# Transposes of a hybrid decoder layer, issued in groups of two tiles with the last formed operand first

## The chip, the cores and the metric

One core of a Trainium2 chip runs the whole layer. The metric is the device time of one execution in microseconds (us).

## What is computed

One macaron layer over 1024 prompt tokens and 64 sample tokens, model width 1024, float32:

```
x = x + 1/2 * post1(SwiGLU_1(pre1(x)))          # width 2816, RMS norms pre and post
h = pre_mix(x); z = h @ w_in + b_in
  A: sliding-window attention, 8 heads on 2 key heads of 64, window 128, learned sinks
  B: HGRN2 gated linear recurrence, 4 heads of 128
x = x + post_mix(concat(norm(attn), gate(hgrn)) @ w_out)
x = x + 1/2 * post2(SwiGLU_2(pre2(x)))
```

## The kernel before

**Tiling.** The tokens go in three blocks: n=0 (256 prompt and 64 sample tokens, width 320), n=1 and n=2 (384 each). A product in float32 is made of three matmuls on operands split into a rounded and a rest part, hi by hi, hi by lo, lo by hi (`mm3`, L245 to L247), 320, 384 or 512 columns wide; these are the large matmuls. Weights come by a DMA that SP issues (L229), and `split` forms hi by a cast on ACT (L222) and lo by a subtraction on DVE (L223). Activations stored in DRAM by the first feed-forward come back in the same way: a DMA `ar<-fa` (L966), the cast and the subtraction `h<-ar` (L222, L223).

**Stages.** Feed-forward 1; then for each block the projection `w_in`, attention and recurrence, the projection `w_out`; feed-forward 2. Feed-forward 2 of block 0 is worked on while blocks 1 and 2 are still mixed: a pair of products is taken through `silu` on ACT (L696) and a product on DVE (L702), which free the two banks.

**Where the transposes stand.** `pre_n` (from L404) normalises a block for the mix and transposes x into feature tiles: eight tiles, each three transposes of 128 x 128 into one PSUM bank `tr` (L428), read out by ACT (L432, hi) and DVE (L433, lo). `pre_s` (from L468) does the same for feed-forward 2 of blocks 1 and 2 (L490; read out by ACT, L495, or DVE, L493, in turn; then a cast of four tiles, L509). `attn_block` (from L1177) works on 128 queries in two passes of two heads of each key head: scores `sc` (L1193), a mask and maximum on DVE (L1201), exponentials on ACT (L1210), then for each key head the transposes of the probabilities into a bank `pT` (L1219, four of 128 x 128, two in the first block), read out by DVE for the first key head and by ACT for the second (L1222), then the product with the values `pv` (L1234). Its result is scaled (L1244) and `finish_attn` squares it on ACT (L1164) and transposes it (`oT`, L1172). `hgrn_block` has its own small products (`kT` L1363, `av` L1368 and L1371, `u` L1374), the squares of `finish_hgrn` (L1339) and the update of the state (L1379).

**What sets the order.** All PSUM is eight banks: four with the tag `mm` for large products, four with the tag `ax` for everything else, each handed out in turn; a writer waits until the last reader of its bank's earlier tile is done. The generators above are advanced between large products by `tick`, `pace` and `stream`: each `yield` ends a slot. The resulting program is then scheduled when it is built (`schedule_with_timeline_sim=True`): a simulated timeline puts the instructions of each engine in order, and on the chip each engine works through its list in that order and waits where an operand or a buffer isn't there. SP's list of DMA issues is such a list too.

Of the kernel before, what the change touches and what calls it, by code (L numbers as in the profile page):

```python
# [8 lines left out]
F32 = mybir.dt.float32  # L9
# [4 lines left out]
AF = mybir.ActivationFunctionType  # L14
ALU = mybir.AluOpType
# [3 lines left out]
P = 128  # L19
D = 1024  # L20
KC = D // P
# [23 lines left out]
def tile_step(ctx: ExitStack, tc: tile.TileContext, A: dict, O: dict):  # L45
    nc = tc.nc
    V, S, G, PE = nc.vector, nc.scalar, nc.gpsimd, nc.tensor
# [8 lines left out]
    def uid(s):  # L56
        cnt[0] += 1
        return f"{s}_{cnt[0]}"
# [4 lines left out]
    def axbank(s="ax"):  # L63
        return ps.tile([P, 512], F32, tag="ax", bufs=4, name=uid(s))
# [5 lines left out]
    def big(dt=F32, shape=(P, 4, 384)):  # L70
        return pp.tile(list(shape), dt, tag="big", bufs=10, name=uid("big"))
# [77 lines left out]
    ident = cp.tile([P, P], F32, name="ident")  # L149
# [68 lines left out]
    def small():  # L218
        return pp.tile([P, 4, 8], F32, tag="small", bufs=10, name=uid("sm"))
# [32 lines left out]
    def hcol(h, k, w):  # L252
        return h[0][k // 4][:, k % 4, :w], h[1][k // 4][:, k % 4, :w]
# [6 lines left out]
    def proj_tok(banks, wt, h, n, ks):  # L260

        for i, bank in enumerate(banks):
            r = rows_of(n, i)
            for k2, k in enumerate(ks):
                hh = hcol(h, k, WIDTH[n])
                mm3(bank[:r], (hh[0][:, i * P:i * P + r], hh[1][:, i * P:i * P + r]),
                    (wt[0][:, k2], wt[1][:, k2]), k == 0, k == KC - 1)

    def rows_of(n, i):
        return min(P, WIDTH[n] - i * P)  # L270

    def new_h(n):
        return [[hslot(n), hslot(n)], [hslot(n), hslot(n)]]
# [130 lines left out]
    def pre_n(n, y, gpre, h):  # L404

        w = WIDTH[n]
        sm = small()
        row_rms(n, y, [0, 1, 2], sm)
        yield
        yield  # L410
        yield
        yield
        for i in range(3):
            r = rows_of(n, i)
            for hf in range(2):
                t = y[hf][:r, i]
                if hf:
                    S.activation(t, t, AF.Copy, scale=sm[:r, 1, i:i + 1])
                else:
                    V.tensor_scalar(t, t, sm[:r, 1, i:i + 1], None, op0=ALU.mult)  # L420
        yield
        yield
        h[n] = new_h(n)
        for d in range(KC):
            bank = axbank("tr")
            for i in range(3):
                r = rows_of(n, i)
                PE.transpose(bank[:, i * P:i * P + r], y[d // 4][:r, i, (d % 4) * P:(d % 4) * P + P],  # L428
                             ident[:r, :r])
            hi, lo = hcol(h[n], d, w)  # L430
            g = gpre[:, d:d + 1]
            S.activation(hi, bank[:, :w], AF.Copy, scale=g)  # L432
            V.scalar_tensor_tensor(lo, bank[:, :w], g, hi.bitcast(F32), op0=ALU.mult, op1=ALU.subtract)  # L433
            if d % 2:
                yield

    def pre_x(n, y, gpre, part, f):

# [29 lines left out]
    def pre_s(n, y, gpre, part, f):  # L468


        sm = small()
        row_rms(n, y, [0, 1, 2], sm)
        yield
        for i in range(3):
            for hf in range(2):
                t = y[hf][:, i]
                if hf:
                    S.activation(t, t, AF.Copy, scale=sm[:, 1, i:i + 1])
                else:
                    V.tensor_scalar(t, t, sm[:, 1, i:i + 1], None, op0=ALU.mult)  # L480
            yield

        part[n] = []
        for kh in range(2):
            a = big()
            part[n].append(a)
            for k in range(4):
                bank = axbank("tr")
                for i in range(3):
                    PE.transpose(bank[:, i * P:(i + 1) * P], y[kh][:, i, k * P:(k + 1) * P], ident)  # L490
                g = gpre[:, 4 * kh + k:4 * kh + k + 1]
                if k % 2:
                    V.tensor_scalar(a[:, k], bank[:, :384], g, None, op0=ALU.mult)  # L493
                else:
                    S.activation(a[:, k], bank[:, :384], AF.Copy, scale=g)  # L495
                yield
            if n == 1:
                yield from factor(f, 1 + kh, a)
        if n == 2:
            yield from factors(n, part, f)  # L500
# [542 lines left out]
    def mixing(tp, h):  # L1043
# [132 lines left out]
        def attn_block(n, b):  # L1176
            zq, kx, vn = Z[n]["q"], KX[n], VN[n]  # L1177
            first = n == 0 and b == 0
            nk = 1 if first else 2
            k0 = P if first else b * P  # L1180
            wk = nk * P
            mask = amask[:, P:] if first else amask
            sm, mx = small(), small()
            ob = None

            def of(x, pr):
                return x.rearrange("p (g r i) -> p g r i", g=2, r=2)[:, :, pr]

            for pr in range(2):
                pt, banks = [], [axbank("sc") for _ in range(2)]  # L1190
                for i in range(2):
                    for g in range(2):
                        PE.matmul(banks[g][:, i * 256:i * 256 + wk],  # L1193
                                  zq[64 * g:64 * g + 64, 2 * pr + i, b * P:(b + 1) * P],
                                  kx[64 * g:64 * g + 64, k0:k0 + wk], start=True, stop=True)
                for g in range(2):
                    p = t2((P, 2, 256))
                    pt.append(p)
                    for i in range(2):
                        hd = 4 * g + 2 * pr + i  # L1200
                        V.tensor_tensor_reduce(out=p[:, i, :wk], in0=banks[g][:, i * 256:i * 256 + wk], in1=mask,  # L1201
                                               op0=ALU.add, op1=ALU.max, scale=1.0, scalar=NEG,
                                               accum_out=mx[:, 0, hd:hd + 1])
                V.scalar_tensor_tensor(of(sm[:, 0], pr), of(mx[:, 0], pr), 0.125, of(sinkb, pr),
                                       op0=ALU.mult, op1=ALU.max)
                V.tensor_scalar(of(sm[:, 1], pr), of(sm[:, 0], pr), -1.0, None, op0=ALU.mult)
                for g in range(2):
                    for i in range(2):
                        hd = 4 * g + 2 * pr + i
                        S.activation(pt[g][:, i, :wk], pt[g][:, i, :wk], AF.Exp, bias=sm[:, 1, hd:hd + 1],  # L1210
                                     scale=0.125, accum_out=mx[:, 1, hd:hd + 1])
                yield
                yield
                pT = []
                for g in range(2):
                    bank = axbank("pT")
                    for i in range(2):
                        for kb in range(nk):
                            PE.transpose(bank[:, (i * nk + kb) * P:(i * nk + kb + 1) * P],  # L1219
                                         pt[g][:, i, kb * P:(kb + 1) * P], ident)  # L1220
                    t = t2()
                    (S.copy if g else V.tensor_copy)(t[:, :2 * wk], bank[:, :2 * wk])  # L1222
                    pT.append(t)
                yield
                if ob is None:
                    ob = axbank("pv")
                for i in range(2):
                    for g in range(2):
                        c = (2 * pr + i) * P + 64 * g
                        for kb in range(nk):  # L1230
                            vb = b + kb + (1 if first else 0)
                            for q0 in (0, 64):
                                k1 = (i * nk + kb) * P + q0
                                PE.matmul(ob[q0:q0 + 64, c:c + 64], pT[g][:, k1:k1 + 64],  # L1234
                                          vn[:, vb, g * 64:g * 64 + 64], start=kb == 0, stop=kb == nk - 1)
                if pr == 0:
                    yield
            V.tensor_tensor(sm[:, 2], sinkb, sm[:, 0], op=ALU.subtract)
            S.activation(sm[:, 2], sm[:, 2], AF.Exp)
            V.tensor_tensor(mx[:, 2], mx[:, 1], sm[:, 2], op=ALU.add)  # L1240
            V.reciprocal(mx[:, 3], mx[:, 2])
            yield
            o = t2()
            V.tensor_tensor(o.rearrange("p (m g d) -> p m g d", m=4, g=2),  # L1244
                            ob.rearrange("p (m g d) -> p m g d", m=4, g=2),
                            mx[:, 3].rearrange("p (g m) -> p m g", g=2).unsqueeze(3).to_broadcast([P, 4, 2, 64]),
                            op=ALU.mult)
            yield from finish_attn(n, o, P, slice(b * P, (b + 1) * P))
# [334 lines left out]
    h = {}  # L1583
# [142 lines left out]
    with tc.tile_pool(name="f2", bufs=1) as tp:  # L1726
# [10 lines left out]
        y, sm = f2.ys[1], small()  # L1737
# [77 lines left out]
```

## Time and profile before

| what | us |
|---|---|
| median of 3 runs | 1953.73 (1953.61 to 1954.24) |
| profiled execution | 1954.31 |
| its span | 1952.6 |
| PE busy | 1937.5 (99%) |
| DVE busy | 1349.6 (69%) |
| ACT busy | 929.0 (48%) |
| POOL busy | 211.1 (11%) |

The profiled execution is 1.7 us longer than the span of its trace, and its mean granted clock of TensorE is 0.998. In the chain of work that ended last, PE has 94%, the rest being DMA 2%, DVE 2%, ACT 1% and issue 1%. In the rows below a line of a timeline begins with the start in us and the duration in us; "x4" is four instructions of one kind in a row, whose duration runs from the first start to the last end. A number in square brackets is the idle time of that engine just before, with what ended it. PE's ends are modelled, so steps from start to start are what counts there. A matmul in full float32 (sc, pv, av, u) shows as two records; a transpose as one.

### The profile page before, as it was taken

What the parts mean: (1) busy time and instruction counts of PE and PEld (TensorE: products, weight loads), DVE (VectorE), ACT (ScalarE), POOL (GpSimd) and SP (SyncE); (2) the same over time, 40 slices, a digit from 0 to 9 for tenths busy, and PEclk for the clock granted to TensorE, in tenths of its full rate; (3) what the DMA queues carried; (4) which work ended last, traced back from release to release, by engine and by line L of the source; (5) the groups of instructions that cost most, each with busy time, mean ns of one, the idle gap of its engine ahead of it and who ended that gap; (6) DMA issues with size and microseconds to landing.
All of it is one profiled execution on the core that took longest, in us unless ns stands there. A gap on an engine that the chain in (4) does not pass through costs nothing.

```text
span 1952.6 us, 34158 instructions
## 1 busy us (share of the span) xinstructions
PE 1937.5 (99%) x13451; PEld 1825.4 (93%) x13451; DVE 1349.6 (69%) x2188; ACT 929.0 (48%) x1637; POOL 211.1 (11%) x213
## 2 busy tenths in 40 slices
PE   9999999999999999999999999999999999999998
PEld 9999999999998987788899898999999999999887
DVE  5876667776558666875667765745987877655666
ACT  6633333444445544654345455745544444444453
POOL 0000000000004112111232431101000000000202
PEclk9999999999999999999999999999999999999999
DMA  9643345556677555675434333556555645577974
GB/s 322 209 143 129 144 162 186 179 183 208 236 236 228 163 146 163 213 228 153 120 101 141 115 112 117 190 166 206 174 204 187 217 177 186 206 237 232 308 260 141
DMA packets 162492, 362.65 MB, mean 186 GB/s; under 512 B 16524, under 2 KB 60236, under 8 KB 162316
## 3 DMA queue, kind: packets, MB, share of 16 engines
q1 hardware_dynamic: 161324, 358.65, 55.5%
q8 instruction: 105, 1.72, 0.4%
q10 hardware_dynamic: 1008, 1.84, 0.3%
q14 instruction: 55, 0.45, 0.1%
HBM read 283.78 MB, written 77.63 MB: 185 GB/s over the span
## 4 chain that ended last, share of the span: by engine, by line
PE 94%; DMA 2%; DVE 2%; ACT 1%; issue 1%; POOL 0%; SPq 0%; DVEq 0%; POOLq 0%; ACTq 0%
PE mm L245 28%; PE mm L247 28%; PE mm L246 28%; PE c L247 1%; PE c L245 1%; PE c L246 1%; DMA ar<-fa 1%; PE pv L1234 1%; PE sc L1193 1%; PE pT L1219 1%; PE lv L1267 0%; DMA raw<-in_ffn_w_gu_dram 0%; DMA x1N<-big 0%; PE av L1368 0%; DMA big<-in_x0T_dram 0%
## 5 line engine op out<-in xcount | busy, mean ns | idle before, releaser
L245 PE MATMUL mm<-h,wsph 128*128 128x320 f32 (+1 forms) x1280 | 409.5, 320 | 0.2 <-DVE sg L702 0.2
L247 PE MATMUL mm<-h,wspl 128*128 128x320 f32 (+1 forms) x1280 | 403.5, 317 | 1.2 <-DVE wspl L223 1.2
L246 PE MATMUL mm<-h,wsph 128*128 128x320 f32 (+1 forms) x1280 | 404.4, 316 | 0.0
L223 DVE TENSOR_TENSOR wspl<-raw,wsph 128x1024 fp32r<-128x1024 f32 x200 | 250.0, 1251 | 156.4 <-ACT wsph L222 156.0
L222 ACT CAST wsph<-raw 128x1024 fp32r<-128x1024 f32 x200 | 209.3, 1048 | 270.6 <-PE mm L246 205.4
L222 ACT CAST w<-raw 128x512 fp32r<-128x512 f32 (+1 forms) x226 | 169.3, 754 | 240.3 <-PE mm L246 119.8
L223 DVE TENSOR_TENSOR w<-raw,w 128x512 fp32r<-128x512 f32 (+1 forms) x226 | 196.6, 874 | 87.8 <-ACT w L222 87.3
L245 PEld LDWEIGHTS mm<-h,wsph 128*128 128x128 f32 x1280 | 240.4, 188 | 5.4 <-issue 3.2
L247 PEld LDWEIGHTS mm<-h,wspl 128*128 128x128 f32 x1280 | 239.9, 188 | 3.0 <-DVE wspl L223 1.7
L246 PEld LDWEIGHTS mm<-h,wsph 128*128 128x128 f32 x1280 | 240.5, 188 | 1.5 <-issue 0.7
L245 PE MATMUL mm<-h,w 128*128 128x384 f32 x704 | 235.6, 335 | 0.0
L246 PE MATMUL mm<-h,w 128*128 128x384 f32 x704 | 235.6, 335 | 0.0
L247 PE MATMUL mm<-h,w 128*128 128x384 f32 x704 | 230.5, 335 | 0.0
L245 PE MATMUL mm<-w,h 128*128 128x512 f32 x462 | 182.2, 398 | 1.9 <-DVE big L979 1.0
L246 PE MATMUL mm<-w,h 128*128 128x512 f32 x462 | 181.0, 392 | 0.0
L247 PE MATMUL mm<-w,h 128*128 128x512 f32 x462 | 178.9, 392 | 0.0
L216 POOL TENSOR_TENSOR sm<-sm,mhalf 128x3 f32<-128x3 f32 (+4 forms) x37 | 33.7, 913 | 1187.6 <-DVE sm L304 462.3
L245 PEld LDWEIGHTS mm<-h,w 128*128 128x128 f32 x704 | 132.2, 188 | 0.2 <-ACT big L793 0.2
L222 ACT CAST w<-t 128x512 fp32r<-128x512 f32 x176 | 107.3, 621 | 52.4 <-PE mm L247 46.9
L246 PEld LDWEIGHTS mm<-h,w 128*128 128x128 f32 x704 | 132.1, 188 | 0.0
L247 PEld LDWEIGHTS mm<-h,w 128*128 128x128 f32 x704 | 131.7, 188 | 0.0
L223 DVE TENSOR_TENSOR w<-t,w 128x512 fp32r<-128x512 f32 x176 | 119.0, 687 | 10.5 <-ACT w L222 10.3
(348 smaller groups left out, 3688.5 us busy)
## 6 DMA issues: line engine op xcount, KB each, us to landing
raw<-in_ffn_w_gu_dram SPq DMA_DIRECT2D x154, 512.0 KB
raw<-in_ffn_w_down_dram SPq DMA_DIRECT2D x74, 512.0 KB
raw<-in_w_in_dram SPq DMA_DIRECT2D x54, 512.0 KB
ar<-fa SPq DMA_DIRECT2D x70, 384.0 KB
big<-in_ffn_w_down_dram SPq DMA_DIRECT2D x88, 256.0 KB
fb<-big SPq DMA_DIRECT2D x44, 512.0 KB
raw<-fb SPq DMA_DIRECT2D x40, 512.0 KB
fa<-big SPq DMA_DIRECT2D x22, 768.0 KB
```

Of the source, the lines that this page charges most:

```text
L216: G.tensor_tensor(y, x, mhalf[:y.shape[0], :y.shape[1]], op=ALU.pow)
L222: formed[1] = S.copy(hi, src)
L223: return (lo_eng or V).tensor_tensor(lo, src, hi.bitcast(F32), op=ALU.subtract)
L245: PE.matmul(out, a[0], b[0], start=first, stop=False, skip_group_check=resume)
L246: PE.matmul(out, a[0], b[1], start=False, stop=False, skip_group_check=resume)
L247: r = latest[0] = PE.matmul(out, a[1], b[0], start=False, stop=last, skip_group_check=resume)
L1193: PE.matmul(banks[g][:, i * 256:i * 256 + wk], zq[64 * g:64 * g + 64, 2 * pr + i, b * P:(b + 1) * P], kx[64 * g:64 * g + 64, k0:k0 + wk], ...
L1219: PE.transpose(bank[:, (i * nk + kb) * P:(i * nk + kb + 1) * P], pt[g][:, i, kb * P:(kb + 1) * P], ident)
L1234: PE.matmul(ob[q0:q0 + 64, c:c + 64], pT[g][:, k1:k1 + 64], vn[:, vb, g * 64:g * 64 + 64], start=kb == 0, stop=kb == nk - 1)
```

## The change

A helper `group` takes a list of transposes and issues them from the last to the first, all but the first with the constraint that they be scheduled behind the one issued first. `pre_n` and `pre_s` take two `tr` banks at once and issue the six transposes of two feature tiles as one group; `attn_block` takes both `pT` banks at once and issues the transposes of both key heads as one group, the second key head first. The reading out is as before, behind the group. In `pre_s` the two yields of a pair now stand together behind it; the number of slots is the same in all three.

```diff
--- before.py
+++ after.py
@@ -266,6 +266,13 @@
                 mm3(bank[:r], (hh[0][:, i * P:i * P + r], hh[1][:, i * P:i * P + r]),
                     (wt[0][:, k2], wt[1][:, k2]), k == 0, k == KC - 1)
 
+    def group(ops):
+        ins = None
+        for out, src, eye in reversed(ops):
+            with tc.issue_after(ins) if ins is not None else nullcontext():
+                r = PE.transpose(out, src, eye)
+            ins = ins or r.ins
+
     def rows_of(n, i):
         return min(P, WIDTH[n] - i * P)
 
@@ -421,18 +428,16 @@
         yield
         yield
         h[n] = new_h(n)
-        for d in range(KC):
-            bank = axbank("tr")
-            for i in range(3):
-                r = rows_of(n, i)
-                PE.transpose(bank[:, i * P:i * P + r], y[d // 4][:r, i, (d % 4) * P:(d % 4) * P + P],
-                             ident[:r, :r])
-            hi, lo = hcol(h[n], d, w)
-            g = gpre[:, d:d + 1]
-            S.activation(hi, bank[:, :w], AF.Copy, scale=g)
-            V.scalar_tensor_tensor(lo, bank[:, :w], g, hi.bitcast(F32), op0=ALU.mult, op1=ALU.subtract)
-            if d % 2:
-                yield
+        for d0 in range(0, KC, 2):
+            banks = [axbank("tr") for _ in range(2)]
+            group([(banks[k][:, i * P:i * P + P], y[d0 // 4][:, i, (d0 % 4 + k) * P:(d0 % 4 + k) * P + P], ident)
+                   for k in range(2) for i in range(3)])
+            for k, bank in enumerate(banks):
+                hi, lo = hcol(h[n], d0 + k, w)
+                g = gpre[:, d0 + k:d0 + k + 1]
+                S.activation(hi, bank[:, :w], AF.Copy, scale=g)
+                V.scalar_tensor_tensor(lo, bank[:, :w], g, hi.bitcast(F32), op0=ALU.mult, op1=ALU.subtract)
+            yield
 
     def pre_x(n, y, gpre, part, f):
 
@@ -484,15 +489,17 @@
         for kh in range(2):
             a = big()
             part[n].append(a)
-            for k in range(4):
-                bank = axbank("tr")
-                for i in range(3):
-                    PE.transpose(bank[:, i * P:(i + 1) * P], y[kh][:, i, k * P:(k + 1) * P], ident)
-                g = gpre[:, 4 * kh + k:4 * kh + k + 1]
-                if k % 2:
-                    V.tensor_scalar(a[:, k], bank[:, :384], g, None, op0=ALU.mult)
-                else:
-                    S.activation(a[:, k], bank[:, :384], AF.Copy, scale=g)
+            for k0 in (0, 2):
+                banks = [axbank("tr") for _ in range(2)]
+                group([(bank[:, i * P:(i + 1) * P], y[kh][:, i, (k0 + k) * P:(k0 + k + 1) * P], ident)
+                       for k, bank in enumerate(banks) for i in range(3)])
+                for k, bank in enumerate(banks):
+                    g = gpre[:, 4 * kh + k0 + k:4 * kh + k0 + k + 1]
+                    if k:
+                        V.tensor_scalar(a[:, k0 + k], bank[:, :384], g, None, op0=ALU.mult)
+                    else:
+                        S.activation(a[:, k0 + k], bank[:, :384], AF.Copy, scale=g)
+                yield
                 yield
             if n == 1:
                 yield from factor(f, 1 + kh, a)
@@ -1211,15 +1218,12 @@
                                      scale=0.125, accum_out=mx[:, 1, hd:hd + 1])
                 yield
                 yield
-                pT = []
+                pT, banks = [], [axbank("pT") for _ in range(2)]
+                group([(banks[g][:, (i * nk + kb) * P:(i * nk + kb + 1) * P], pt[g][:, i, kb * P:(kb + 1) * P], ident)
+                       for g in range(2) for i in range(2) for kb in range(nk)])
                 for g in range(2):
-                    bank = axbank("pT")
-                    for i in range(2):
-                        for kb in range(nk):
-                            PE.transpose(bank[:, (i * nk + kb) * P:(i * nk + kb + 1) * P],
-                                         pt[g][:, i, kb * P:(kb + 1) * P], ident)
                     t = t2()
-                    (S.copy if g else V.tensor_copy)(t[:, :2 * wk], bank[:, :2 * wk])
+                    (S.copy if g else V.tensor_copy)(t[:, :2 * wk], banks[g][:, :2 * wk])
                     pT.append(t)
                 yield
                 if ob is None:
```

In the changed kernel the lines lie lower down: the transposes are L273, the reading out L438, L439, L499, L501 and L1226, `ar<-fa` L973, silu L703, pv L1238.

The order of the instructions on all engines is the same in both kernels up to about 824 us of the timeline of before, but for the reversed order inside the groups, and again from about 1420 us on. The number of matmuls is the same. Counted over PE's whole order, the runs of small matmuls between large ones go from 147 to 126.

The first place is at about 829 us, where a product of feed-forward 1 that is still open takes a stored activation (`h_1142`, from the load `ar_1143`) while weights of `w_in` (`raw_1184`) are loaded. SP's DMA issues, before and now:

```order
L966 DMA ar_1128_8081<-fa1_101 128x2x384
L229 DMA raw_1166_8354<-in_w_in_dram 128x1024
L229 DMA raw_1179_8414<-in_w_in_dram 128x1024
L966 DMA ar_1143_8160<-fa1_101 128x2x384
L229 DMA raw_1184_8449<-in_w_in_dram 128x1024
L377 DMA gb_1170_8376<-in_norm_ffn1_post_dram 128x512
L966 DMA ar_1150_8203<-fa1_101 128x2x384
```

```order
L973 DMA ar_1128_8081<-fa1_101 128x2x384
L229 DMA raw_1166_8354<-in_w_in_dram 128x1024
L229 DMA raw_1179_8414<-in_w_in_dram 128x1024
L229 DMA raw_1184_8449<-in_w_in_dram 128x1024
L973 DMA ar_1143_8160<-fa1_101 128x2x384
L384 DMA gb_1170_8376<-in_norm_ffn1_post_dram 128x512
L973 DMA ar_1150_8203<-fa1_101 128x2x384
```

The load of `ar_1143` has changed places with the weight load `raw_1184`. ACT at the same place, before and now (tr are `pre_n`'s transposed tiles, av is the recurrence's output, t2_1159 attention's):

```order
L432 ACTIVATE h_1115_8055<-tr_1144_8182,cols_78 128x384
L432 ACTIVATE h_1115_8055<-tr_1145_8188,cols_78 128x384
L222 CAST h_1142_8159<-ar_1143_8160 128x2x384
L1339 ACTIVATE big_898_6608,sm_1153_8263<-av_1151_8245 128x128 x4
L1164 ACTIVATE junk_73,sm_1160_8302<-t2_1159_8300 128x512
L222 CAST h_1149_8202<-ar_1150_8203 128x2x384
L222 CAST h_1157_8277<-ar_1158_8278 128x2x384
```

```order
L438 ACTIVATE h_1115_8055<-tr_1145_8183,cols_78 128x384
L438 ACTIVATE h_1115_8055<-tr_1144_8182,cols_78 128x384
L1343 ACTIVATE big_898_6608,sm_1153_8263<-av_1151_8245 128x128 x4
L1171 ACTIVATE junk_73,sm_1160_8302<-t2_1159_8300 128x512
L222 CAST h_1142_8159<-ar_1143_8160 128x2x384
L222 CAST h_1149_8202<-ar_1150_8203 128x2x384
L222 CAST h_1157_8277<-ar_1158_8278 128x2x384
```

The cast of `h_1142` stands behind the four squares and attention's square instead of ahead of them. PE's matmuls there stand as they stood.

The second place is at about 1283 us, in feed-forward 2 of block 0 (`mm_1872`, `mm_1873`, `mm_1881`: products of 320 columns; `sg_1865`: silu of the pair before them; `wsph`: hi part of a weight tile; `h_1870`: cast of four transposed tiles of block 1). ACT, before and now:

```order
L222 CAST wsph_1867_13311<-raw_1866_13309 128x1024
L1222 COPY t2_1855_13234<-pT_1854_13229 128x512
L495 ACTIVATE big_1845_13179<-tr_1856_13236,cols_78 128x384
L222 CAST wsph_1875_13358<-raw_1874_13356 128x1024
L696 ACT_TABLE_LOAD
L696 ACTIVATE sg_1865_13307<-mm_1857_13243 128x320
L1164 ACTIVATE junk_73,sm_1863_13297<-t2_1862_13295 128x512
L509 CAST h_1870_13334<-big_1845_13179 128x1536
L222 CAST wsph_1879_13390<-raw_1878_13388 128x1024
L696 ACTIVATE sg_1877_13386<-mm_1872_13354 128x320
```

```order
L222 CAST wsph_1879_13390<-raw_1878_13388 128x1024
L1226 COPY t2_1855_13234<-pT_1853_13223 128x512
L222 CAST wsph_1884_13424<-raw_1883_13422 128x1024
L501 ACTIVATE big_1845_13179<-tr_1856_13236,cols_78 128x384
L516 CAST h_1870_13334<-big_1845_13179 128x1536
L703 ACT_TABLE_LOAD
L703 ACTIVATE sg_1865_13307<-mm_1858_13248 128x320
L703 ACTIVATE sg_1877_13386<-mm_1872_13354 128x320
L1171 ACTIVATE junk_73,sm_1864_13302<-t2_1863_13300 128x512
```

The silu `sg_1865` stood right behind the eviction of a tr tile and one cast; now `wsph_1884`, the eviction and the cast of `h_1870` are ahead of it, and two silus follow each other. PE up to the first matmul of `mm_1881`, before and now:

```order
L246 MATMUL mm_1873_13355<-h_1560_11096,wsph_1860_13247 128x320
L247 MATMUL mm_1873_13355<-h_1558_11094,wspl_1861_13248 128x320
L245 MATMUL mm_1873_13355<-h_1558_11094,wsph_1860_13247 128x320
L246 MATMUL mm_1873_13355<-h_1560_11096,wsph_1860_13247 128x320
L247 MATMUL mm_1873_13355<-h_1558_11094,wspl_1861_13248 128x320
L1172 MATMUL oT_1869_13327<-ident_66,t2_1862_13295 128x128 x4
L245 MATMUL mm_1881_13420<-h_1557_11093,wsph_1867_13311 128x320
L246 MATMUL mm_1881_13420<-h_1559_11095,wsph_1867_13311 128x320
```

```order
L273 MATMUL pT_1853_13223<-ident_66,t2_1844_13170 128x128 x4
L273 MATMUL pT_1852_13222<-ident_66,t2_1843_13167 128x128 x4
L273 MATMUL tr_1857_13237<-ident_66,big_1698_12302 128x128 x3
L245 MATMUL mm_1873_13355<-h_1558_11094,wsph_1861_13252 128x320
L246 MATMUL mm_1873_13355<-h_1560_11096,wsph_1861_13252 128x320
L247 MATMUL mm_1873_13355<-h_1558_11094,wspl_1862_13253 128x320
L273 MATMUL tr_1856_13236<-ident_66,big_1698_12302 128x128 x3
L1238 MATMUL pv_1835_13109<-vn_1409_10193,t2_1854_13232 64x64 x4
L1238 MATMUL pv_1835_13109<-vn_1409_10193,t2_1855_13234 64x64 x4
L1238 MATMUL pv_1835_13109<-vn_1409_10193,t2_1854_13232 64x64 x4
L1238 MATMUL pv_1835_13109<-vn_1409_10193,t2_1855_13234 64x64 x4
L245 MATMUL mm_1881_13420<-h_1557_11093,wsph_1867_13311 128x320
```

Before, all 48 matmuls of `mm_1872` and `mm_1873` and one run of oT stood between the last tr transposes and `mm_1881`; now those products are nearly done when the groups come, and three large matmuls, the run of `tr_1856` and pv are all that lies between the last cast's release and `mm_1881`.

## Rows read from the trace of the kernel before

**Rows 1.** Page, section 1: busy us of each engine (share of the span), instructions

```profile
PE 1937.5 (99%) x13451; PEld 1825.4 (93%) x13451; DVE 1349.6 (69%) x2188; ACT 929.0 (48%) x1637; POOL 211.1 (11%) x213
```

**Rows 2.** Waits of PE over the whole span: us in total, times, longest

```profile
PE lv L1267 <- DVE big L1316: 2.1, 1, 2.1
PE tr L428 <- DVE h L433: 0.9, 1, 0.9
PE mm L245 <- ACT h L222: 0.9, 1, 0.9
```

**Rows 3.** Timeline of PE, start and us, around runs of four and of one

```profile
683.57 0.60 PE L1219 MATMUL pT<-ident,t 128*128 128x128 f32 x4
683.93 0.39 PE L245 MATMUL mm<-h,wsph 128*128 128x320 f32 x1
684.16 0.30 PE L246 MATMUL mm<-h,wsph 128*128 128x320 f32 x1
...
1348.05 0.31 PE L247 MATMUL mm<-h,wspl 128*128 128x320 f32 x1
1348.20 0.27 PE L490 MATMUL tr<-ident,big 128*128 128x128 f32 x1
1348.45 0.31 PE L246 MATMUL mm<-h,wsph 128*128 128x320 f32 x1
```

**Rows 4.** Stretches (PE, PEld, DVE, ACT, POOL, PEclk, DMA), then timeline of PE

```profile
750.00:760.00 10.00, 6.95 (x79) 5.15 (x80) 8.79 (x13) 5.04 (x8) 2.80 (x5) 0.66 0.61 184
818.00:819.00 1.00, 0.28 (x1) 0.28 (x2) 1.00 (x3) 1.00 (x2) 0.26 (x1) 1.00 0.79 315
...
755.31 0.80 PE L245 MATMUL mm<-w,h 128*128 128x512 f32 x1 [1.03 <-DVE big L979]
```

**Rows 5.** Timelines of SP, ACT and PE, 822 to 833 us

```profile
822.52 0.39 SPq L966 DMA_DIRECT2D ar<-fa  x1
825.35 0.33 SPq L229 DMA_DIRECT2D raw<-in_w_in_dram  x1
827.22 2.86 SPq L966 DMA_DIRECT2D ar<-fa  x2
...
827.49 0.83 ACT L222 CAST h<-ar 128x768 fp32r<-128x768 f32 x1
829.73 0.65 ACT L1164 ACTIVATE junk<-t 128x512 bf16<-128x512 f32 x1
832.36 0.83 ACT L222 CAST h<-ar 128x768 fp32r<-128x768 f32 x1 [1.89 <-DMA ar<-fa]
...
829.33 0.48 PE L245 MATMUL mm<-w,h 128*128 128x512 f32 x1
```

**Rows 6.** Timelines of ACT and PE, 1272 to 1284 us

```profile
1272.44 0.59 ACT L495 ACTIVATE big<-tr,cols 128x384 f32<-128x384 f32 x1
1274.48 1.05 ACT L222 CAST wsph<-raw 128x1024 fp32r<-128x1024 f32 x1 [1.45 <-issue]
1275.54 1.28 ACT L696 ACT_TABLE_LOAD   x1
1276.84 0.44 ACT L696 ACTIVATE sg<-mm 128x320 f32<-128x320 f32 x1
1278.12 1.46 ACT L509 CAST h<-big 128x1536 fp32r<-128x1536 f32 x1
...
1283.33 0.39 PE L245 MATMUL mm<-h,wsph 128*128 128x320 f32 x1
```

**Rows 7.** Timeline of PE, 1138 us: the values product of a block

```profile
1138.60 1.15 PE L1234 MATMUL pv<-vn,t 128*64 128x64 f32 x32 [0.75 <-DVE t L1222]
```

**Rows 8.** Timelines of DVE and PE behind the scores, 1264 us

```profile
1264.65 0.42 DVE L1201 CUSTOM_DVE_ANT_0 t<-sc,amask 128x256 f32<-128x256 f32 x1 [1.26 <-PE sc L1193]
1265.34 0.08 DVE L1201 DVE_READ_ACCUMULATOR2_ANT sm<- 128x1 f32 x1
...
1264.55 0.55 PE L490 MATMUL tr<-ident,big 128*128 128x128 f32 x3
```

## The prediction

> **What bounds the kernel now.** I read the busy shares first, then PE's waits, then PE's timeline around runs of transposes, then the two orders side by side, and last the timelines of ACT, SP and DVE where the orders part. PE is busy for 1937.5 of 1952.6 us [rows 1], so a change can win only by taking work off PE or one of its few waits, and it loses whatever PE newly waits. The longest waits after the start-up are one of 2.1 us for DVE (L1316), one of 0.9 for a feature tile (L428 behind DVE L433) and one of 0.9 for an activation half-tile (ACT L222) [rows 2], one of 1.03 at 755.31 [rows 4], and 0.75 at 1138.60 for a copy of a pT bank [rows 7]. The rest of the span is matmul behind matmul.
>
> The profiled execution took 1954.31 us, 0.58 above the median of 1953.73; I sum against 1954.31. A measurement of this kernel can tell about 0.2%, 3.9 us, from no change.
>
> **What grouping can save on PE.** The change issues the same transposes in the same number, 126 runs of small matmuls between large ones where 147 stood (counted over the two orders), and fewer waits. A run of one costs this: it starts at 1348.20, the second large matmul behind it at 1348.45, and of these 0.25 us a large matmul takes 0.15 itself (1348.05 to 1348.20), so 0.10. A run of four: 683.57 to 684.16, 0.59 less 0.15, so 0.44, or 0.11 each [rows 3]. The price per transpose is the same in a short and in a long run. A joint run saves nothing by its length: 0. If the slot of 0.23 instead of 0.15 us that the first large matmul behind a run takes (683.93 to 684.16) were a price of its own, 21 runs at 0.08 would be 1.7 us; the run of one speaks against it, since its whole excess is 0.10. That is the bound on the gain side.
>
> Starting with the last formed operand means that the first transpose of a group waits for everything and the rest for nothing. The waits it replaces were mostly satisfied when PE came to them, so this too is 0, except where PE reaches the group early. At the last attention block (about 1132 us) that happens: four runs that followed the exponentials one by one now wait for the last. Its cover is the 0.75 us at 1138.60, where pv waits for a DVE copy whatever PE did before [rows 7]; up to that size the earlier wait is taken out of the later one. I take 0. Without that cover it would be below 0.75.
>
> Up to about 824 us the order on all engines is the same but for the reversals inside groups. So the waits at 749, 755, 815 and 818 stay, and nothing is won there. From there to about 1420 us the scheduler has laid the instructions otherwise, and the question is where that hurts. I went through PE's matmuls in the new order, asking for each wait whether its producer's place in its own queue, with durations from the trace, comes before or after PE. Three places remain.
>
> **A, 829 us: the load of ar_1143 goes behind raw_1184 on SP.** Before, it was issued at 822.52, and raw_1184 at 825.35 because it waits for a buffer [rows 5]. Now the wait of raw_1184 stands ahead of it, so it goes out at about 825.7. The next load of this kind was issued at 827.22 and ended an idle time of ACT at 832.36, 5.1 us later [rows 5]; the moved one itself was there by 827.49, at most 5.0 after its issue. That makes a landing at 830.7 at the latest. Its cast on ACT (0.83 us, 827.49 before) is now also queued behind the four squares and L1164, which end at 829.73 + 0.65 = 830.4 [rows 5]. So the cast starts between 830.4 and 830.8 and ends between 831.3 and 831.7. PE's first matmul with it stood at 829.33 [rows 5]. PE waits 1.9 to 2.4 us; I take **2.0**, as the earlier of the two limits is a queue that the trace shows and the later one a longest latency. The DVE half comes 0.9 us behind the cast and is wanted seven matmuls (1.6 us) later: 0. The later `ar` loads stand on SP where they stood, behind it and a gain row, and their casts have the idle time of ACT before 832.36 ahead of them (1.89 us) [rows 5].
>
> **C, 1265 us: the pair of tr banks stands right behind the scores.** In the new order PE has the four sc matmuls, then two runs of three. The second run takes a bank that DVE must first read out (two L1201 operations): the first starts at 1264.65, the second ends at 1265.34 + 0.08, so the bank is free at about 1265.4. PE reached its first run at 1264.55 and three transposes take 0.33, so it would be at the second at 1264.9 [rows 8]. It waits about **0.6**; 0 if PE comes there later, 0.9 if one more such operation (0.35) is ahead on DVE.
>
> **D, 1283 us: the silu that frees a bank moves behind a cast, an eviction and the table load.** Four mm banks rotate. Matmul mm_1881 writes the bank that silu sg_1865 has read. Before, silu ran at 1276.84 and mm_1881 at 1283.33, 6 us later [rows 6]. Now mm_1881 is issued right after the last of a tr group and pv, and silu follows on ACT a cast of a weight tile, the eviction of that tr group, the cast of h_1870 and the table load. ACT: 1.05 + 0.59 + 1.46 + 1.28 + 0.44 = 4.8 us [rows 6], less about 0.1 of overlap at some joints. The first of them waits for a matmul that PE ends some 0.2 us after it starts its last large matmul. PE from there: 0.15 for that matmul, 0.33 for three transposes, 1.15 for pv x32 [rows 7], so 1.6 to 1.7. PE waits 0.2 + 4.6 - 1.7 = **3.1**. If the weight cast were out of the way, the chain would start with the eviction, after the transposes: 0.6 + 3.7 - 1.7 = 2.6. If nothing overlaps, 3.4.
>
> The Trainium skill (ScalarE: Activation LUTs, What ACT_TABLE_LOAD costs) gives a switch of tables a drain of about 1.38 us beside the load's 1.28. Here the load begins at 1275.54, as the cast before it ends (1274.48 + 1.05), and silu runs at 1276.84, right behind it [rows 6]: no drain is seen, the trace decides, and I use 1.28. By the page D would be 4.5 and the time 1963.5.
>
> **The clock.** After the 2.1 us wait at 752 the granted clock was 0.5: 0.66 in the mean of 750 to 760 means 6.8 of 10 us at 1.2 GHz [rows 4]. Counted from about 752.8, just behind that wait, they end at about 759.6. From PE's return for good at 755.31 [rows 4] that is 4.3 us at half rate, 2.1 us lost. The two waits of 0.9 around 815 to 819 left it at 1.00 [rows 4]. D is longer than the wait that cost the clock, A about equal to it. I count one loss, **2.1**, and give the number of losses its own cases: 0, 1 or 2.
>
> Sum: 2.0 + 0.6 + 3.1 + 2.1 = 7.8, so 1954.3 + 7.8 = **1962.1**, 7.8 us or 0.4% above the profiled execution. Nothing behind 1290 us can take it up: PE has no idle time there to be shortened. After D, what is late next is the silu of the following pair and the casts behind it on ACT; they are wanted a whole pair of banks later.
>
> **The rivals.**
> 1. The waits come, the clock holds: 1954.3 + 5.7 = 1960.0. For it: the waits of 0.9 did nothing. Against: D is 1 us longer than one that did.
> 2. The clock falls at A and at D: 1964.2. For it: A is 2.0 us against 2.1, and PE comes to both waits from short transposed and 64-column work. [...]
> 3. No change that can be measured, about 1954.3 to 1957: the change does not do what it says or nothing hangs on it. The order keeps several groups of three apart, with other work between; if ACT runs some 3 us further ahead at D than I place it, D goes, and A alone is below 0.2%. For it: ACT is busy only 48% [rows 1]. Against: each of its operations there waits for PE, by the new order.
> 4. Faster: the wait at 752 goes, with the clock loss that follows and the 1.03 at 755. They are worth 2.1 + 2.1 + 1.0 = 5.2 [rows 2, 4], and without A and D this gives 1949.1. It decides if DVE comes to L1316 more than 2 us sooner, as evictions of a pair end closer together. Against: DVE's order up to there is the same, and with A to D beside it the sum is 1954.8, which is rival 3.
>
> **How the numbers follow.** Forecast 0.36, rival 1 0.25, rival 2 0.11, rival 3 0.21, rival 4 0.07. Slower by over 0.2% (above 1957.6) is the forecast with rivals 1 and 2: 0.72; within, rival 3: 0.21; faster 0.07. The range reaches from 1955, which takes in the low ends (1.9 + 0 + 2.6 gives 1958.8) and the upper part of rival 3, to 1965.5, which takes in rival 2 with D at 3.4 and C at 0.9 and leaves out rival 4 and the rest of 3.
>
> **What would show it.** Right: among PE's waits a new one of about 2 us, mm (L245) on ACT h (L222), near 829; one of about 3 us, mm (L245) on ACT sg (L703), near 1290 by the new time; 0.6 us of tr on DVE near 1270; a granted clock of 0.5 for some us behind one of them; and the same waits at 749 to 819. A run of four or eight transposes still costs 0.11 us each. Wrong: no wait over 1 us behind 824, or PE's large matmuls following a joint run sooner than 0.10 us per transpose.

## The result, and the profile after

| | median us | runs | range |
|---|---|---|---|
| before | 1953.61 | 5 | 1950.23 to 1954.24 |
| after | 1961.15 | 5 | 1960.01 to 1962.26 |

The change makes the kernel slower: the medians are 7.5 us apart, and the ratio is 1.0046, with a 95% interval of 1.0035 to 1.0057. The forecast was 1962.1 in a range of 1955 to 1965.5. The profiled execution took 1961.28 us with a span of 1959.6, 7.0 more than before. PE is busy for 1939.8 us of it, against 1937.5 [rows 1], so 4.7 of the 7.0 us are idle time of PE.

The waits of PE over the whole span of the changed kernel (in total, times, longest), to be laid beside [rows 2]:

```profile
PE mm L245 <- ACT h L222: 3.4, 2, 2.5
PE mm L245 <- ACT sg L703: 3.4, 1, 3.4
PE mm L245 <- DVE big L986: 1.4, 1, 1.4
PE tr L273 <- DVE h L439: 1.3, 1, 1.3
...
PE pT L273 <- ACT t L1217: 0.4, 1, 0.4
PE tr L273 <- DVE sm L1208: 0.4, 1, 0.4
```

The wait for ACT h has a second occurrence of 2.5 us (A), the wait for silu sg is new (D), the wait of tr for L1208 is new (C), and so is the one of pT for the last exponential, at the block where the prediction put it at no net cost. And the 2.1 us for L1316 of [rows 2] is missing.

A in the timelines of SP, ACT and PE after, to be laid beside [rows 5]:

```profile
822.96 0.33 SPq L229 DMA_DIRECT2D raw<-in_w_in_dram  x1
823.34 0.96 SPq L973 DMA_DIRECT2D ar<-fa  x1
...
827.39 0.64 ACT L1171 ACTIVATE junk<-t 128x512 bf16<-128x512 f32 x1
828.87 0.83 ACT L222 CAST h<-ar 128x768 fp32r<-128x768 f32 x1 [0.75 <-DMA ar<-fa]
...
829.75 0.50 PE L245 MATMUL mm<-w,h 128*128 128x512 f32 x1 [2.52 <-ACT h L222]
```

The load goes out behind raw_1184 and takes 5.5 us (823.34 to 828.87). ACT is through with the square at 828.1 and then idles for the load. So the load ended last here, not ACT's queue.

D in the timelines of ACT and PE after, beside [rows 6]:

```profile
1283.73 1.05 ACT L222 CAST wsph<-raw 128x1024 fp32r<-128x1024 f32 x1 [0.52 <-PE mm L246]
1284.68 0.57 ACT L501 ACTIVATE big<-tr,cols 128x384 f32<-128x384 f32 x1
1285.29 1.47 ACT L516 CAST h<-big 128x1536 fp32r<-128x1536 f32 x1
1286.78 1.28 ACT L703 ACT_TABLE_LOAD   x1
1288.07 0.77 ACT L703 ACTIVATE sg<-mm 128x320 f32<-128x320 f32 x2
...
1284.06 1.15 PE L1238 MATMUL pv<-vn,t 128*64 128x64 f32 x32
1288.56 0.42 PE L245 MATMUL mm<-h,wsph 128*128 128x320 f32 x1 [3.36 <-ACT sg L703]
```

PE is done with pv at about 1285.2 and waits until the first of the two silus, 3.4 us. The load of the table again follows the cast without a gap and takes 1.28 us.

What the clock did, in three stretches after (columns as in [rows 4]; the third number from the end is the granted clock):

```profile
750.00:760.00 10.00, 8.59 (x98) 6.69 (x97) 7.92 (x11) 5.19 (x8) 5.02 (x9) 1.00 0.64 199
...
815.00:825.00 10.00, 10.00 (x76) 8.27 (x77) 7.11 (x12) 4.41 (x8) 0.00 (x0) 0.85 0.30 82
...
1285.00:1295.00 10.00, 6.64 (x41) 6.50 (x38) 5.32 (x8) 5.61 (x9) 0.55 (x1) 0.83 0.28 85
```

Behind D the clock fell to its lower level: 0.83 over 10 us is 1.7 us of full speed lost. At 752, where [rows 4] had 0.66, it stayed at 1.00 this time. Around 815 to 819, where it had stayed at 1.00 [rows 4], it fell as well: 0.85 over 10 us is 1.5 us lost. The prediction had no fall there; the experiments come back to it.

A run of eight transposes after, beside [rows 3]:

```profile
1265.97 0.31 PE L247 MATMUL mm<-h,wspl 128*128 128x320 f32 x1
1266.12 1.03 PE L273 MATMUL pT<-ident,t 128*128 128x128 f32 x8
1266.91 0.39 PE L245 MATMUL mm<-h,wsph 128*128 128x320 f32 x1
1267.14 0.31 PE L246 MATMUL mm<-h,wsph 128*128 128x320 f32 x1
```

From 1266.12 to 1267.14 is 1.02 us, less 0.15 for the large matmul is 0.87, 0.11 each. The longer run saves nothing, as forecast.

### The profile page after: what moved, and what is told of

The parts are those of the page before. It is cut to its first block, busy times and chain, and to the rows that moved or that the text cites. A ratio compares the mean times of both kernels' runs of the same rounds, so it can differ in the third digit from the quotient of the medians.

```text
span 1959.6 us, 34146 instructions
## 1 busy us (share of the span) xinstructions
PE 1939.8 (99%) x13451; PEld 1826.7 (93%) x13451; DVE 1349.5 (69%) x2188; ACT 929.0 (47%) x1637; POOL 214.9 (11%) x213
## 4 chain that ended last, share of the span: by engine, by line
PE 93%; DMA 3%; DVE 2%; ACT 1%; issue 1%; POOL 0%; SPq 0%; DVEq 0%; POOLq 0%; ACTq 0%
PE mm L245 28%; PE mm L247 28%; PE mm L246 28%; PE c L247 1%; PE c L245 1%; PE c L246 1%; DMA ar<-fa 1%; PE pv L1238 1%; PE sc L1200 1%; PE pT L273 1%; PE lv L1271 0%; DMA raw<-in_ffn_w_gu_dram 0%; PE tr L273 0%; DMA x1N<-big 0%; DMA big<-in_x0T_dram 0%
```

## The experiments

Eleven kernels ran, each beside runs of the kernel before on the same chip. The medians of before there were 1951.1 to 1951.7 us, 2 us lower than in the first comparison; before_again bears on that.

**One part of the change alone.** pn_only has only the hunk of `pre_n` (and `group`), pt_only only that of `attn_block`, ps_only only that of `pre_s`.

> Only pre_n grouped and reversed; pre_s and attn_block as before. Queue theory (the loss comes from the places A, C and D in the engines' orders): this kernel has A's order (the load of ar_1143 behind raw_1184, its cast behind the squares) and not D's, so PE waits about 2.0 to 2.5 us for ACT h at 829 and nothing at 1283: +2.5 us, +4.2 if the clock falls there. Rival (grouping itself costs, in proportion to the groups: 8 of 32 are here): a quarter of the 7.5 us, +1.9, with no single wait.

Measured: 1956.82 us, ratio 1.0027 (1.0015 to 1.0039), +5.2 us. The waits of PE, and the stretch with its granted clock:

```profile
PE mm L245 <- ACT h L222: 4.1, 2, 3.2
...
825.00:835.00 10.00, 6.80 (x28) 5.42 (x27) 5.33 (x12) 4.29 (x14) 1.53 (x2) 0.83 0.43 141
```

A alone, 3.2 us here, and the clock falls behind it (1.7 us). No other new wait. The rival's +1.9 without a single wait is out.

> Only attn_block's pT of both key heads grouped and reversed. Queue theory: D's order without A's: a wait of 2.7 to 3.4 us of mm (L245) for sg near 1283, none at 829; with the clock falling once behind it (1.7 us) +4.4 to +5.1, without +2.7 to +3.4. Rival (in proportion, 16 of 32 groups): half of 7.5, +3.7, with no single wait over 1 us.

Measured: 1958.41 us, ratio 1.0032 (1.0022 to 1.0043), +6.8 us. PE's wait:

```profile
PE mm L245 <- ACT sg L703: 3.5, 1, 3.5
```

D alone, with the clock at 0.83 behind it: 3.5 + 1.7 is 5.2 of the 6.8. The rival's +3.7 without a wait over 1 us is out. Its profile also has the clock falling at 815 to 820, as that of the change has and those of pn_only and ps_only have not.

> Only pre_s grouped and reversed. Queue theory: neither A nor D; C alone, a wait of about 0.4 us for DVE behind the scores near 1265: +0.4, not to be told from no change. Rival (in proportion, 8 of 32 groups): +1.9.

Measured: 1951.85 us, ratio 1.0001 (0.9993 to 1.0010). No change, as the queue theory had it and the rival not. C, which was expected here with 0.4 us, isn't among its waits of PE, and pt_only has 0.2 us of it, so C doesn't come from `pre_s` alone. Its order is that of before up to far behind 752; there its profile has no wait for L1316, and:

```profile
750.00:760.00 10.00, 8.40 (x97) 6.49 (x96) 8.58 (x12) 5.20 (x8) 4.50 (x7) 1.00 0.68 197
```

**The groups, issued forward.**

```diff
-        for out, src, eye in reversed(ops):
+        for out, src, eye in ops:
```

> The whole change, but each group issued from the first to the last, so the same two-tile groups without the last formed operand first. Its order has neither A (ar_1143 stays ahead of raw_1184) nor D (silu sg_1865 stays ahead of the cast of h_1870). Queue theory: 0 to +0.5 us against before, no new wait over 0.5 us. Rival (grouping itself costs): +7.5 as the change. Second rival (the reversal saves on PE and only the queues spoil it): a run of eight transposes takes more than 0.11 us each here than in the change.

Measured: 1950.12 us, ratio 0.9995 (0.9987 to 1.0004). With the first formed operand first, the groups cost nothing. Its waits of PE hold none of A, C and D:

```profile
PE mm L245 <- ACT h L222: 0.9, 1, 0.9
PE pv L1238 <- DVE t L1226: 0.8, 1, 0.8
PE tr L273 <- DVE h L439: 0.7, 1, 0.7
```

Its groups stay whole where all operands are there, and part where they come one by one. PE's timeline at a group of each kind:

```profile
1044.05 1.03 PE L273 MATMUL pT<-ident,t 128*128 128x128 f32 x8
1044.84 0.42 PE L245 MATMUL mm<-h,wsph 128*128 128x384 f32 x1
1045.10 0.34 PE L246 MATMUL mm<-h,wsph 128*128 128x384 f32 x1
...
1252.94 0.38 PE L273 MATMUL pT<-ident,t 128*128 128x128 f32 x2
...
1254.34 0.38 PE L273 MATMUL pT<-ident,t 128*128 128x128 f32 x2
```

The whole group takes 1044.05 to 1045.10 less 0.17, 0.88 us or 0.11 each, so the second rival is out: the reversal saves nothing on PE. The other stands in four runs of two, the first and the last shown, with large matmuls between. Two banks held at once are no price, then. The price comes with the reversal, which makes PE begin a group when its last operand is formed, and the next three kernels ask whether it comes through the order that the scheduler then writes.

**The reversal kept, the queues mended.** cure_A holds the weight loads behind the last `ar` load on SP; cure_D holds the cast behind the last silu on ACT; cure_A_and_D does both.

```diff
@@ cure_A, load_w and act
-            nc.sync.dma_start(raw if sl is None else raw[sl], ap)
+            with tc.issue_after(lastar[0]) if lastar[0] is not None else nullcontext():
+                nc.sync.dma_start(raw if sl is None else raw[sl], ap)
...
-                nc.sync.dma_start(raw[:, :n], FA[:, k0:k0 + n, SLOT[m]])
+                lastar[0] = nc.sync.dma_start(raw[:, :n], FA[:, k0:k0 + n, SLOT[m]]).ins
@@ cure_D, factor and gated0
-        S.copy(hi, src)
+        with tc.issue_after(silu[0]) if silu[0] is not None else nullcontext():
+            S.copy(hi, src)
...
-                S.activation(t[:, :w], g[:, :w], AF.Silu)
+                silu[0] = S.activation(t[:, :w], g[:, :w], AF.Silu).ins
```

> The whole change, and the weight loads are held behind the last load of ar on SP, so that ar_1143 is issued ahead of raw_1184 and its cast stands ahead of the squares, as before the change; D's order stays. Queue theory: the wait of 2.5 us at 829 is gone, the one of 3.4 for sg stays: 2.5 us below the change (4.2 with a fall of the clock behind A), so +4 to +5 against before, as with pT alone. Rival (the reversal costs by itself, wherever the queues stand): no difference to the change, +7.5 to +9.

Measured: 1959.01 us, ratio 1.0039 (1.0027 to 1.0052), +7.9 us.

```profile
PE mm L247 <- ACT sg L705: 3.4, 1, 3.4
...
PE mm L247 <- ACT h L222: 0.4, 1, 0.4
```

A is gone and D stays. The gain of 2.5 us that was expected is not in the median: it is 0.7 us nearer to before than that of change_again (+8.6) and no nearer than that of the first comparison (+7.5). The profiled execution is the slowest of its five; in it the clock fell at 815 to 825 (0.67 in the mean), which takes the gain back in the table below.

> The whole change, and the cast of four transposed tiles is held behind the last silu on ACT, so that the table load and sg_1865 come ahead of the cast of h_1870; A's order stays. Queue theory: the wait for sg shrinks by that cast, from 3.4 to about 1.9 us, and the clock stays or falls as before: 1.5 us below the change without a difference of the clock, 3.2 with one. Rival (the wait is ACT's load as a whole, not the place in the queue): the wait stays at 3 us or more.

Measured: 1959.26 us, ratio 1.0042 (1.0029 to 1.0054), +8.1 us.

```profile
PE mm L246 <- ACT h L222: 3.1, 2, 2.2
PE mm L246 <- ACT sg L705: 1.9, 1, 1.9
...
1285.00:1295.00 10.00, 8.15 (x76) 8.01 (x71) 6.46 (x9) 6.42 (x11) 0.55 (x1) 1.00 0.36 104
```

D shrinks to 1.9 us by the cast that is out of the way, and the clock behind it holds at 1.00. The wait is a matter of the place in ACT's queue, not of ACT's load. By the medians the gain is only 0.5 us of the 3.2 that wait and clock make. With 95% intervals of about 2.5 us to either side the medians of the cures don't decide. Their profiles do, for D: in the table below, the stretch between the columns 1222 and 1307 adds 2.6 us in cure_D and 2.5 in cure_A_and_D, and 5.6, 5.6 and 5.5 in after, change_again and cure_A, so about 3.0 us of wait and clock are gone there. The profile of cure_D has lost 1.5 us before that, at 752 (before_again, below). For A the table doesn't decide: the stretch between 771 and 856 adds 3.1 us in cure_A and 1.6 in cure_A_and_D, some 4 in after and 1.6 in change_again, and the clock's fall at 815 lies in the same stretch. That A's wait costs its time rests on pn_only and on the lists of waits.

> Both of the two cures on the whole change. Queue theory: no wait at 829, about 1.9 us for sg: 4 to 6 us below the change, +2 to +4 against before. Rival (reversal costs by itself): +7.5 or more.

Measured: 1956.83 us, ratio 1.0027 (1.0014 to 1.0039), +5.7 us, where 2 to 4 was expected. Both waits are as expected (1.9 for sg, none at 829), so some of the loss is not in A, C and D. To find it I took the start of the same large matmul (by its number among PE's 10242) in each profile, less its start in ps_only:

```
large matmul no.      4400   4700   4900   6250   6700  last
its start, ps_only   771.0  855.9  903.0 1221.8 1306.7 1941.9
before                 3.8    3.2    3.2    3.3    3.3    3.5
before_again           4.4    4.4    4.4    4.4    4.4    5.5
forward               -0.5   -1.4   -1.4   -1.4   -1.4   -0.7
pn_only               -0.7    4.6    5.8    5.9    5.9    7.0
pt_only               -0.5    1.7    1.7    1.8    7.9    8.1
cure_A                 0.4    3.5    4.7    4.8   10.3   10.6
cure_D                 1.5    4.1    5.4    5.4    8.0    8.4
cure_A_and_D           0.4    2.0    3.2    3.3    5.8    6.3
after                 -0.4    3.6    4.8    4.9   10.5   10.5
change_again          -0.4    1.2    2.4    2.5    8.1    8.4
```

Between the columns 771 and 856 lie A and what the clock does around 815; between 1222 and 1307 lie C and D. Between 856 and 903 there is a step of 1.2 us that no list of waits shows. Exactly the five kernels with the reversed groups of `pre_n` have it, the change in both of its profiles, and none of the others. PE's timeline there, after:

```profile
891.98 1.12 PE L1503 MATMUL su<-t,m 32*128 32x512 f32 x2
893.03 0.44 PE L247 MATMUL mm<-h,wspl 128*128 128x384 f32 x1
...
896.36 1.12 PE L1503 MATMUL su<-t,m 32*128 32x512 f32 x2
897.41 0.44 PE L247 MATMUL mm<-h,wspl 128*128 128x384 f32 x1
```

and in ps_only:

```profile
888.46 1.13 PE L1508 MATMUL su<-t,m 32*128 32x512 f32 x4
889.51 0.44 PE L247 MATMUL mm<-h,wspl 128*128 128x384 f32 x1
```

The two `su` matmuls of the sample recurrence use 32 rows of the array each, at different rows. One behind the other they run side by side and take 1.05 us together (888.46 to 889.51). In the new order 18 large matmuls stand between them, and each takes 1.05 us by itself (891.98 to 893.03, 896.36 to 897.41). I call this E: +1.2 us with the change back to large matmuls. Bringing the pair together again, with the reversal kept, was not tried on the chip, so E rests on the step in the table and on these lines.

With E, 5.1 of the cured kernel's +5.7 have a place: 1.9 for sg, 0.4 for C, 1.2 for E and some 1.6 between the columns 771 and 856, where its clock fell at 815 to 820 (0.83 in the mean of 815 to 825). That fall is in four of the seven profiles with a reversed group ahead of 815 (pt_only, cure_A, cure_A_and_D, after) and in none of the four without one; whether the reversal brings it or chance does is left open.

**The noise.** before_again is the kernel before; change_again is the change.

> The kernel before, unchanged, profiled once more. Theory: the wait of 2.1 us for L1316 at 752 and the fall of the clock behind it belong to that one execution (they were not seen in any kernel since, with the same order up to there), so its profile shows no wait of 2 us at 752 and a span about 4 us shorter than 1952.6. Rival: they belong to the kernel before, and the change in the groups ahead of 749 took them away: the wait and the half clock are there again.

Measured: 1952.36 us, ratio 1.0005 (0.9996 to 1.0014). Its profiled execution was its slowest, 1956.35 us:

```profile
PE lv L1267 <- DVE big L1316: 2.1, 1, 2.1
...
750.00:760.00 10.00, 6.52 (x79) 4.64 (x78) 8.47 (x13) 5.48 (x9) 2.46 (x5) 0.69 0.56 175
```

By this profile alone the rival is right: the wait is there again. But ps_only, forward and before_look2 (below) have the same order there and have it not, and the runs of before on this chip go from 1949.5 to 1956.5. What differs is the arrival of a load that ACT waits for, first here, then in ps_only:

```profile
749.56 0.83 ACT L222 CAST h<-ar 128x768 fp32r<-128x768 f32 x1 [5.15 <-DMA ar<-fa]
```

```profile
747.37 0.83 ACT L222 CAST h<-ar 128x768 fp32r<-128x768 f32 x1 [3.46 <-DMA ar<-fa]
```

The cast starts 5.1 us behind the issue of that load here (744.47) and 3.4 us in ps_only (743.97). So the loss belongs to single executions: a load that comes late, 2.1 us of waiting and the clock behind it, some 4 us together (column 771: 3.8 and 4.4). Both profiles of before hit it, neither of the change did, and cure_D's has 0.6 us of the wait with the clock at 0.83 in the mean of 750 to 760.

> The change, unchanged, profiled once more beside the runs of before on the same chip. Theory: the waits A (2 to 3 us at 829), C (0.4) and D (3.4) and the torn pair of su matmuls near 893 (1.2) are there again; the fall of the clock behind D is there if that is a matter of D's length, and may be missing behind A and at 815; +8 to +10 against before. Rival (the result is one of several layouts of chance): one of the three waits is missing.

Measured: 1960.22 us, ratio 1.0045 (1.0033 to 1.0058), +8.6 us. C and D and the torn pair are there unchanged, and the clock behind D (0.83). A is 1.7 us this time:

```profile
821.85 0.43 SPq L973 DMA_DIRECT2D ar<-fa  x1
...
825.89 0.65 ACT L1171 ACTIVATE junk<-t 128x512 bf16<-128x512 f32 x1
826.41 0.22 ACT L1171 ACTIVATION_READ_ACCUMULATOR junk<-t 128x1 f32 x1
826.51 0.84 ACT L222 CAST h<-ar 128x768 fp32r<-128x768 f32 x1
```

Here the load was there within 4.7 us (821.85 to 826.51) and the cast follows the square at once, so the queue on ACT ended last, as I had taken it in the prediction. A varies with the load: 1.7, 2.2, 2.5 and 3.2 us in the four profiles with its order (change_again, cure_D, after, pn_only), where the cast starts 4.7, 5.3, 5.5 and 6.2 us behind the issue of the load.

**A version that is faster than both.** The waits around 815 to 819 are in every profile so far, and I took them for a late `ar` load. The two kernels here load these tiles two ahead outside the inner part, too.

```diff
-            AC[ms] = Ahead([lambda m=m, ks=ks: act(m, ks) for m in ms for ks in GROUPS], 2 if inner else 1)
+            AC[ms] = Ahead([lambda m=m, ks=ks: act(m, ks) for m in ms for ks in GROUPS], 2)
```

> The forward groups, and the stored activations of the pairs outside the inner part (ar) are loaded two ahead instead of one, which brings the load for the matmul that waits for ACT h near 818 forward on SP. Theory (those waits of DVE h and ACT h around 815 to 819, 0.7 to 2.3 and 0.9 us in every profile so far, are the load's lateness): both go, and with them the fall of the clock that some executions have there: -1.5 to -3 us against before, so the fastest of all. Rival (the buffers that the early load takes are missed elsewhere): the waits move to another place and the time is as before.

> The kernel before with the loads two ahead and no grouping. As forward_look2: -1.5 to -3 us against before by the theory, and equal to forward_look2 within 1 us, since grouping costs and saves nothing on PE; if grouping forward saved something by itself, this one is slower than forward_look2 by more than 1 us.

Measured: 1948.93 and 1948.94 us, both 0.9987 of before (0.9978 and 0.9979 to 0.9996), -2.7 us. The longest wait is now the same in both, 1.4 us, and those for DVE h and ACT h are gone or down to 0.3. First that of forward_look2, then that of before_look2:

```profile
PE mm L245 <- DVE big L986: 1.4, 1, 1.4
```

```profile
PE mm L245 <- DVE big L979: 1.4, 1, 1.4
```

So loading further ahead takes these waits away, but that the load was late is not shown: before, the engine that idles ahead of the cast at 817.85 is ACT, 1.3 us for POOL (L995) and not for a load, and the earlier load also gives that cast another place in ACT's list. That the two kernels are equal says once more that the forward groups neither cost nor save anything.

## Why the prediction was right

The forecast was slower by over 0.2%, with 0.72, at 1962.1 us. The measured 0.46% has that sign and size. Step by step:

- **Nothing saved by grouping, 0:** right. 0.11 us per transpose in a run of eight; forward equal to before, and before_look2 to forward_look2.
- **The pT wait at the last block, 0 net:** right. It appeared with 0.42 us and the 0.75 of [rows 7] went; the table moves by 0.1 between 903 and 1222.
- **A, 2.0 (1.9 to 2.4):** right in place and cause, the size 2.5 in the profile and 1.7 to 3.2 over the kernels. The step that was off is "the earlier of the two limits is a queue that the trace shows": the load may come after it, and took 5.5 us where [rows 5] had at most 5.1.
- **C, 0.6:** 0.4, in place.
- **D, 3.1 (2.6 to 3.4):** 3.4, the end where nothing overlaps, and it goes to 1.9 without the cast. The 1.4 us of drain that the Trainium skill (ScalarE: Activation LUTs, What ACT_TABLE_LOAD costs) adds to a switch of tables is not in this trace either.
- **The clock, one loss of 2.1:** one fall behind D, of 1.7 us, and in this profile a second one at 815 to 819, where the prediction had none. The one behind D came in all four profiles with 3.4 to 3.5 us of wait, and in neither of the two with 1.9. Behind A it fell once in four, at 3.2 us; that was rival 2.
- **"Three places remain":** wrong by one. E, 1.2 us, stands in PE's new order and I passed it, since I had gone through the order for waits and not for matmuls that lose a neighbour.
- **"So the waits at 749, 755, 815 and 818 stay":** wrong for the one at 752 as this execution shows, though not by the change, and so not by rival 4. I took the profiled execution as typical, but some 4 us of it belong to that execution. The time came out right because the base and the clock's term were too high where A, D and E were too low or missing; that it came within 1 us is luck, while the sign, the places A, C and D and their causes are not.

With what was measured: A 2.5, C 0.4, D 3.4, the clock 1.7, E 1.2 make 9.2 us. That is about what the ratios give (1.0045 and 1.0046, 8.8 to 9.0 us); by the medians it is 8.6 and 7.5, and A alone goes from 1.7 to 2.5 us between the two profiles of the change. Between the two profiled executions only 7.0 are left, since before had 4.2 more at 752 (3.8 against -0.4 in the table), and the change some 2 us more at 815 to 819, where its clock fell (between the columns 771 and 856 it gains 3.9, of which A is 2.5, and before loses 0.6).

## What to carry to other kernels

A change that only reorders operations on the bottleneck is read in the order of all queues: find, for each wait of the bottleneck, where its producer now stands in its own queue, with durations from the trace. Look in the same pass for small matmuls that ran side by side and are now apart, which no list of waits shows. And before a sum is made against one profiled execution, ask which of its waits hang on a load's arrival: a second profile of the same kernel, or of one with the same order there, tells what is chance.

## What was not expected of the hardware

Two matmuls of 32 rows at different rows of the array took 1.05 us together and 1.05 us each when 18 large matmuls stood between them. The Trainium skill (TensorE: Matmul & The Clock Gate, Part 3: Packing small matmuls) describes such tiles as running at once in one array; the trace agrees (1.05 us for both), and adds that here it was lost where the order parted them. And the same load of 384 KB, issued in the same order, was there within 4.7 us in one execution of the change and took 5.5 in the other; a wait that hangs on it is no constant of the kernel.
